# A gate product with tokens as the stationary operand, its nonlinearity in halves, a new order in the last step of a sweep, and an earlier split of one output chunk

## The chip, the cores and the metric

The kernel runs on one core of one Trainium2 chip. The metric is the device time of one execution in microseconds (us). Three timed executions of the kernel before took 1257.67, 1259.69 and 1261.07 us; their median is 1259.69. A further execution was recorded by the hardware profiler, and its trace is what the readings below come from.

Engines: PE is TensorE (matmuls), DVE is VectorE, ACT is ScalarE, POOL is GpSimd, SP is SyncE, which here only issues DMAs.

## What is computed

One encoder layer over 2048 tokens of width 1024 (batch 1). A joint projection feeds two groups of heads, gated linear attention (GLA, both directions) and latent attention (MLA); both are multiplied by a SiLU gate, concatenated, projected, and added to the residual before a layer norm. Cut to what the change touches:

```python
def hybrid_mixer(x, positions, w_in, ..., w_out):
    h = x @ w_in
    (g_q, g_k, g_v, g_gate, g_lr_f, g_lr_b,
     m_cq, m_ckv, m_kr, m_gate) = jnp.split(h, idx, axis=-1)
    o_a = gla_branch(g_q, g_k, g_v, g_gate, ...)      # 512 wide, 4 heads, chunks of 64
    o_b = mla_branch(m_cq, m_ckv, m_kr, m_gate, ...)  # 512 wide, 4 heads
    return jnp.concatenate([o_a, o_b], axis=-1) @ w_out

def mla_branch(c_q, c_kv, k_rope, gate, positions, ...):
    q = (rms_norm(c_q, q_norm_g) @ w_uq).reshape(B, S, 4, 128 + 64)
    kv = (rms_norm(c_kv, kv_norm_g) @ w_ukv).reshape(B, S, 4, 128 + 128)
    ...                                   # rotary parts, dense softmax attention
    return o * jax.nn.silu(gate)

x = layer_norm(DEEPNORM_ALPHA * x + mixed, ln_g, ln_b)
```

Inputs and result are float32. Every large product is made of three passes on operands that are split in a high and a low part (high x high, high x low, low x high); names that end in h and l are these parts.

## The kernel before

The rows of x are 16 chunks of 128 tokens. The kernel has these stages, with the times at which they lie in the profiled execution:

- **The first sweep** (0 to 349 us) goes over the chunks from the last to the first, for the GLA's projections and one direction of its scan. The change does not touch it.
- **The second sweep** (349 to 580 us), `sweep_c`, has 8 steps of two chunks. Each step makes, for both chunks, the MLA projections (`ipm`), the normalised `cq` and `ckv`, their transposes (`tm`), the rotary query `pqr`, the other GLA direction (`Ob`, `og`, `oT`), the absorbed query `pq`, and the gate product `pz` of 512 columns (`c_pz`).
- **The attention** (580 to some 1077 us): 16 blocks, each a head and 512 queries, about 30 us a block.
- **The output** (from some 1060 us): 16 chunks of 128 rows. Each has to be fetched (`OutProj.load`), split into high and low parts (`hi` on ACT, `lo` on POOL), multiplied by the gate (`gate`), multiplied by `w_out`, added to the residual and normalised (`finish`). The layer norm's logarithm and exponential are on ACT.

**The gate product.** `c_pz` computes z transposed: the stationary operand is a block of 128 x 128 of the weights Wz, the moving one the 256 tokens of the step, so that a PSUM tile [128 features, 4 heads, 256 tokens] is filled. A step has 4 heads x 8 slices of the width x 3 passes = 96 matmuls of 128x256, in 8 pieces (n = 0 to 7), which the tables place among the other work. Then `c_gm1` to `c_gm3` (ACT: exp(-z), ln(1 + that), exp of minus that) and `c_gm4` (DVE: times z) make the SiLU on the whole tile (128x1024) in one go, into the SBUF tile `gm`, and `c_sgm` stores it to the scratch `gm_s`. The tile `gm` and the low part of the absorbed query, `qal`, have the same tag and so take turns in one buffer: `gm`'s first writer waits until the store `ql_s<-qal` has landed.

**PSUM.** `pz`, `Ob` and `pq` take turns in the two tiles of the tag "gp". A wait between engines is set per tile, not per part of a tile.

**What sets the order.** For the second sweep every piece of work has a place in a table: `PLACE_C`, with `PLACE_C_FIRST` and `PLACE_C_LAST` for the first and last step. A place is a number of steps after the step's start; where there are two, they are for the step's two chunks. `put` adds step and place, all is sorted by the sum, and `in_order` then fixes that order on each engine:

```python
def put(n, st, fn, *a, j=None):
    last = st == len(steps) - 1
    p = PLACE_C[n]
    p = (last and PLACE_C_LAST.get(n)) or (not st and PLACE_C_FIRST.get(n)) or p
    todo.append((st + (p if j is None else p[j]), len(todo), fn, a))
```

The attention has a sorted list of the same kind. In the output the order in the code is fixed for ACT, POOL and SP (`fixed`), not for PE and DVE. There, `split(c + 2)`, `load(c + 4)`, `product`, `finish` follow each other for each chunk c from 4 on. The work `turn` and `rows` of the last block but one (a turned row of softmax sums, which ACT copies as `rt` to go to the scratch r_s) stands after chunk 6's `finish`.

The GLA's output goes to DRAM as `oa_s`, turned in blocks of 32x32, and `load` puts the blocks in their places with four DMAs for each chunk (`blocks_of`).

Of the kernel before, what the change touches and what calls it, by code (L numbers as in the profile page):

```python
# [9 lines left out]
F32 = mybir.dt.float32  # L10
# [125 lines left out]
STEP_C = ("gm1", "gm2", "gm3", "gm4", "sgm", "pq", "qah", "qal", "sqa")  # L136
# [3 lines left out]
    "ss", "rgl", "rgd", "og", "oT", "soT")  # L140
# [57 lines left out]
    gm1=0.823,  # L198
    gm2=0.832,
    gm3=0.837,  # L200
    gm4=0.845,
# [72 lines left out]
    gm1=0.643,  # L274
    gm2=0.815,
    gm3=0.82,
    gm4=0.83,
# [14 lines left out]
    pqr=(0.749, 1.284),  # L292
    tq=(0.95, 2.1),
    xh=(-0.262, -0.109),
    sqO=(0.15, 0.435),
    rgl=(0.229, 0.457),
    sqm=(0.101, 0.657),
    rml=(0.187, 0.878),
    cq=(0.463, 1.041),
    ckv=(0.35, 1.075),  # L300
# [6 lines left out]
    oT=(0.337, 0.509),  # L307
    oib=(0.063, 0.43),
    ss=(0.166, 0.454),
    rgd=(0.332, 0.461),  # L310
    og=(0.336, 0.508),
    ssm=(0.1025, 0.733),
    rmd=(0.29, 1.022),
    krf=(0.139, 0.6),
    cqTl=(0.598, 1.211),
    ckvTl=(0.88, 1.703),
    qrf=(0.795, 1.556),
    qrTl=(1.081, 2.186),
    xl=(-0.244, 0.3),
# [6 lines left out]
    qrfa=(0.871, 2.029),  # L326
# [3 lines left out]
    lu=(0.281, 0.47),  # L330
# [3 lines left out]
    gm1=1.309,  # L334
    gm2=1.608,
    gm3=1.859,
    gm4=1.953,
# [16 lines left out]
class K:  # L354
# [151 lines left out]
    def run(self):  # L506
        tc, nc, ins = self.tc, self.nc, self.ins
        with ExitStack() as top:
# [9 lines left out]
            self.gm_s = [dp.tile([P, H, QB], F32, name=f"gm_s{b}") for b in range(NQB)]  # L518
# [3 lines left out]
            self.kt_s = [dp.tile([P, H, P], F32, name=f"kt_s{c}") for c in range(NCH)]  # L522
            self.r_s = [dp.tile([1, H, QB], F32, name=f"r_s{b}") for b in range(NQB)]
# [627 lines left out]
    def sweep_c(self):  # L1151


        with ExitStack() as ctx:
# [102 lines left out]
    def c_pz(self, s, n):  # L1257
        last = s["st"] == NCH // 2 - 1
        if n == 0:
            s["pz"] = self.gp.tile([P, H, 256], F32, tag="gp", name=f"pz{s['st']}")  # L1260
        order = [(h, k) for h in range(H) for k in range(NK)]
        if last:
            order = [(h, k) for p in range(2) for k in range(NK) for h in (p, p + 2)]
        x2 = lambda t, k: t[:, k].rearrange("p a t -> p (a t)")
        part = [(h, k, p) for h, k in order[4 * n:4 * n + 4] for p in range(3)]
        if n == 0 and s["st"]:

            part.sort(key=lambda e: e[2] == 1)
        stop = {h: (k, p) for h, k, p in part if k == NK - 1}
        for h, k, p in part:  # L1270
            w, x = ((0, self.xch), (0, self.xcl), (1, self.xch))[p]
            self.nc.tensor.matmul(s["pz"][:, h], self.Wz[k][w][:, h * P:(h + 1) * P], x2(x, k),  # L1272
                                  start=(k == 0 and p == 0), stop=stop.get(h) == (k, p))

    def c_gm1(self, s):
        s["gm"] = self.w1.tile([P, H, 256], F32, tag="gm", name=f"gm{s['st']}")
        self.nc.scalar.activation(s["gm"], s["pz"], AF.Exp, scale=-1.0)

    def c_gm2(self, s):
        self.nc.scalar.activation(s["gm"], s["gm"], AF.Ln, bias=1.0)  # L1280

    def c_gm3(self, s):
        self.nc.scalar.activation(s["gm"], s["gm"], AF.Exp, scale=-1.0)

    def c_gm4(self, s):
        self.nc.vector.tensor_tensor(s["gm"], s["pz"], s["gm"], ALU.mult)
# [4 lines left out]
    def c_sgm(self, s):  # L1291
        b, qs = self.of_step(s)
        self.nc.sync.dma_start(self.gm_s[b][:, :, qs], s["gm"])
# [825 lines left out]
```

## Time and profile before

| | us |
|---|---|
| median of three timed executions | 1259.69 (1257.67 to 1261.07) |
| profiled execution, its own time | 1264.79 |
| span of the profiled execution | 1262.9 |
| PE busy | 1239.1 |
| DVE busy | 896.3 |
| ACT busy | 729.1 |
| POOL busy | 726.5 |

How such a page is read: busy times are of one engine and overlap with the others; an engine with idle time may still hold up another. The views used below are: the chain of waits (from the last instruction back to what released each step), the list of what an engine waited for (total, times, longest), windows (busy time of every engine in a stretch of the span, with PE's granted clock as a share of full speed and the DMA engines' mean busy share), groups of instructions (engine, operation, tile written <- tile read, shape, count, then busy time, mean in ns, idle time before and what ended it), the timeline (start, length, engine, line, operation, and in brackets the idle time before it and what ended that), and DMA groups (count, KB each, us from issue to landing). PE's matmuls are pipelined, so the time of one in a run is the distance from its start to the next one's, not its listed length.

### The profile page before, as it was taken

The numbers are of one execution on the slowest core, as the hardware profiler recorded it, in microseconds if no ns is written. First come the engines' busy times: TensorE is split into PE (matmuls) and PEld (weight loads), VectorE is DVE, ScalarE is ACT, GpSimd is POOL, SyncE is SP. The second block draws the span as 40 slices with busy tenths as digits, with TensorE's granted clock in tenths as the row PEclk, the third lists the DMA queues.
The fourth block names the chain that finished last, engine by engine and source line by source line (L and its number), as shares of the span: only waits on it lengthen the run. The fifth ranks groups of instructions, "written<-read, shape, count | busy, mean of one in ns | idle before, by whom it ended". The sixth has DMA issues, their size and how long they took to land.

```text
span 1262.9 us, 19554 instructions
## 1 busy us (share of the span) xinstructions
PE 1239.1 (98%) x6848; PEld 1089.6 (86%) x6848; DVE 896.3 (71%) x1666; ACT 729.1 (58%) x1149; POOL 726.5 (58%) x443
## 2 busy tenths in 40 slices
PE   7999999999999999999999999999999999999997
PEld 7999999999899999988788888888888888887886
DVE  6635454554565666665899999999999998378767
ACT  6643434444564444544888888888888888411210
POOL 0132323232355556530798888889999999935551
PEclk9999999999999999999999999999999999999999
DMA  8225555555757788868412222202234110487773
GB/s 294 68 84 130 134 143 139 144 139 144 266 180 212 212 247 244 245 184 210 79 28 49 43 50 43 53 15 59 59 93 93 41 42 26 125 206 212 198 210 100
DMA packets 277393, 165.59 MB, mean 131 GB/s; under 512 B 178630, under 2 KB 234830, under 8 KB 277296
## 3 DMA queue, kind: packets, MB, share of 16 engines
q1 hardware_dynamic: 276176, 162.23, 48.3%
q0 software_dynamic: 672, 2.10, 0.4%
q8 instruction: 54, 0.88, 0.3%
q14 instruction: 43, 0.35, 0.1%
q10 hardware_dynamic: 448, 0.03, 0.0%
HBM read 105.54 MB, written 58.75 MB: 130 GB/s over the span
## 4 chain that ended last, share of the span: by engine, by line
PE 84%; DVE 4%; DMA 4%; POOL 2%; issue 2%; ACT 2%; SPq 1%; DVEq 0%; POOLq 0%; ACTq 0%
PE pz L1272 7%; PE ipm L1341 5%; PE pS L1605 5%; PE pS L1607 4%; PE pS L1606 4%; PE pS L1608 4%; PE pS L1609 4%; PE o L421 4%; PE o L419 4%; PE o L420 4%; PE ipa L419 4%; PE ipa L421 4%; PE ipa L420 4%; PE ipg L421 2%; PE ipg L419 2%
## 5 line engine op out<-in xcount | busy, mean ns | idle before, releaser
L371 POOL TENSOR_TENSOR pl<-s,ph 128x1024 fp32r<-128x1024 f32 x128 | 306.8, 2416 | 47.2 <-ACT ph L365 37.0
L1614 ACT ACTIVATE s<-pS 128x1024 f32<-128x1024 f32 x128 | 131.5, 1028 | 52.9 <-PE pS L1609 49.0
L1627 DVE TENSOR_TENSOR rm<-pS,rm 128x512 f32<-128x512 f32 x210 | 144.6, 689 | 18.3 <-ACT s L1614 12.7
L1651 DVE TENSOR_TENSOR s<-s,mb 128x1024 f32<-128x1024 f32 x128 | 151.2, 1213 | 9.0 <-PE mb L1645 8.9
L365 ACT ACTIVATE ph<-s 128x1024 fp32r<-128x1024 f32 x128 | 134.8, 1056 | 15.7 <-PE o L421 15.1
L1655 ACT ACTIVATE s<-s 128x1024 f32<-128x1024 f32 x128 | 131.6, 1051 | 10.3 <-DVE s L1651 9.6
L419 PE MATMUL ipa<-wah,xah 128*128 128x384 f32 (+1 forms) x384 | 129.2, 336 | 6.1 <-ACT wah L365 6.1
L420 PE MATMUL ipa<-wal,xah 128*128 128x384 f32 (+1 forms) x384 | 125.0, 325 | 0.0
L421 PE MATMUL ipa<-wah,xal 128*128 128x384 f32 (+1 forms) x384 | 124.7, 325 | 0.0
L1091 POOL TENSOR_TENSOR Sb<-Sb,Us 64x512 f32<-64x512 f32 x15 | 19.9, 1327 | 171.5 <-DVE Us L1083 162.3
L1605 PE MATMUL pS<-qh,kvT 128*128 128x512 f32 x256 | 102.6, 401 | 0.8 <-DVE rm L1627 0.4
L419 PE MATMUL o<-ph,vh 128*128 128x512 f32 x256 | 100.9, 394 | 0.0
L1607 PE MATMUL pS<-qh,kvT 128*128 128x512 f32 x256 | 100.0, 391 | 0.0
L1606 PE MATMUL pS<-ql,kvT 128*128 128x512 f32 x256 | 100.0, 390 | 0.0
L421 PE MATMUL o<-ph,vl 128*128 128x512 f32 x256 | 99.8, 390 | 0.0
L1608 PE MATMUL pS<-rh,kvT 128*128 128x512 f32 x256 | 99.8, 390 | 0.0
L1609 PE MATMUL pS<-rl,kvT 128*128 128x512 f32 x256 | 99.8, 390 | 0.0
L420 PE MATMUL o<-pl,vh 128*128 128x512 f32 x256 | 99.7, 389 | 0.0
L1678 DVE TENSOR_TENSOR ap<-ap,s 128x512 f32<-128x512 f32 x120 | 82.9, 691 | 2.7 <-ACT s L1655 0.7
L419 PEld LDWEIGHTS ipa<-wah,xah 128*128 128x128 f32 x384 | 73.3, 191 | 9.3 <-ACT wah L365 6.4
L371 POOL TENSOR_TENSOR ol<-of,oh 128x512 fp32r<-128x512 f32 x32 | 42.5, 1328 | 59.8 <-ACT oh L365 47.4
L1272 PE MATMUL pz<-xch,wzh 128*128 128x256 f32 x256 | 73.4, 290 | 1.4 <-DVE og L1529 1.3
(308 smaller groups left out, 3404.9 us busy)
## 6 DMA issues: line engine op xcount, KB each, us to landing
xcf<-xT_dram SPq DMA_DIRECT2D x16, 512.0 KB, 5.5
xr<-x_dram SPq DMA_DIRECT2D x16, 512.0 KB, 6.0
out_dram<-rr SPq DMA_DIRECT2D x32, 256.0 KB, 3.5
xaf<-xT_dram SPq DMA_DIRECT2D x14, 512.0 KB, 4.2
oib<-oi_s SPq DMA_DIRECT2D x16, 256.0 KB, 4.9
qdb<-qd_s SPq DMA_DIRECT2D x16, 256.0 KB, 3.5
SU<-su_s SPq DMA_DIRECT2D x16, 256.0 KB, 5.0
ub<-u_s SPq DMA_DIRECT2D x16, 256.0 KB, 4.1
```

Of the source, the lines that this page charges most:

```text
L371: return e.tensor_tensor(dst, src, hi.bitcast(F32), ALU.subtract).ins
L419: mm(out, ah, bh, start=start, stop=False)
L420: mm(out, ah, bl, start=False, stop=False)
L421: mm(out, al, bh, start=False, stop=stop)
L1272: self.nc.tensor.matmul(s["pz"][:, h], self.Wz[k][w][:, h * P:(h + 1) * P], x2(x, k), start=(k == 0 and p == 0), stop=stop.get(h) == (k, p))
L1605: mm(ps[:, e], kh, qh, start=True, stop=False)
L1606: mm(ps[:, e], kh, ql, start=False, stop=False)
L1607: mm(ps[:, e], kl, qh, start=False, stop=False)
L1608: mm(ps[:, e], kr, rh, start=False, stop=False)
L1609: mm(ps[:, e], kr, rl, start=False, stop=True)
L1627: V.tensor_tensor(d["rm"], src[:, e], d["rm"], ALU.max)
L1651: V.tensor_tensor(s, s, d["mb"][:, None, :].to_broadcast([P, 2, QB]), ALU.subtract)
```

## The change

Six things change together.

1. `c_pz` computes z with tokens in rows. The stationary operand is a chunk's x (128 x 128), the moving one 512 columns of Wz. One half of the tile [128, 2, 512] belongs to each chunk; a step has 48 matmuls of 128x512. Pieces 0 to 3 are the first chunk, 4 to 7 the second.
2. `gm1` to `gm4` are pieces of a chunk, not of a step: each works on 128x512. `gm4` writes its product back to PSUM, and a new DVE piece `gmx` transposes it in blocks of 32x32 into `gm`.
3. `qal` is two tiles of 128x512 under another tag, "og", with two DVE instructions and two stores, and no longer shares `gm`'s buffer.
4. `gm_s` gets the layout of `oa_s`. A new function `place_blocks` copies, during the attention, both from DRAM to a new DRAM scratch `og_s`, with eight DMAs for each chunk, in which the 32x32 blocks are put in their places. `load` then takes one DMA for each of the two instead of four and one.
5. The last step's table has new places for `rml`, `rmd`, `ssm`, `sqm`, `cq`, `ckv`, `oib`, `sqO`, `ss`, `rgl`, `rgd`, `og`, `oT`, `pqr`, `qrf`, `krf`, `lu` and `xl`, and a table `PLACE_C_PRE` changes some of the step before.
6. In the output, chunk 6 is split ahead of chunk 3's `finish`, and `turn` and `rows` of the last block but one stand ahead of chunk 6's `finish`.

```diff
@@ tables
+PLACE_C_PRE = dict(
+    cqTl=(0.758, 1.185),
+    tq=(1.44, 1.56),
...
+    soT=(1.119, 1.3),
+)
-STEP_C = ("gm1", "gm2", "gm3", "gm4", "sgm", "pq", "qah", "qal", "sqa")
+STEP_C = ("sgm", "pq", "qah", "qal", "sqa")
@@ PLACE_C
-    gm1=0.823,
+    gm1=(0.45, 0.823),
...
+    gmx=(0.76, 0.835),
@@ PLACE_C_LAST
-    rml=(0.187, 0.878),
-    cq=(0.463, 1.041),
+    rml=(0.187, 0.535),
+    cq=(0.4275, 0.61),
...
@@ scratch
-            self.gm_s = [dp.tile([P, H, QB], F32, name=f"gm_s{b}") for b in range(NQB)]
+            self.gm_s = [dp.tile([2, H, P, P], F32, name=f"gm_s{s}") for s in range(NCH // 2)]
+            self.og_s = [dp.tile([P, 2, H, P], F32, name=f"og_s{c}") for c in range(NCH)]
@@ put
-                p = PLACE_C[n]
+                p = st == len(steps) - 2 and PLACE_C_PRE.get(n) or PLACE_C[n]
@@ c_pz
-            s["pz"] = self.gp.tile([P, H, 256], F32, tag="gp", name=f"pz{s['st']}")
...
-        for h, k, p in part:
-            w, x = ((0, self.xch), (0, self.xcl), (1, self.xch))[p]
-            self.nc.tensor.matmul(s["pz"][:, h], self.Wz[k][w][:, h * P:(h + 1) * P], x2(x, k),
-                                  start=(k == 0 and p == 0), stop=stop.get(h) == (k, p))
+            s["pz"] = self.gp.tile([P, 2, 512], F32, tag="gp", name=f"pz{s['st']}")
+        j, half = divmod(n, 4)
+        for k in (2 * half, 2 * half + 1):
+            xh, xl = self.xch[:, k, j], self.xcl[:, k, j]
+            self.mm3(s["pz"][:, j], xh, xl, self.Wz[k][0], self.Wz[k][1], start=(k == 0), stop=(k == NK - 1))
@@ gate
+    def gm(self, d):
+        s, j = d["step"], d["j"]
+        if "gm" not in s:
+            s["gm"] = self.w1.tile([P, 2, 512], F32, tag="gm", name=f"gm{s['st']}")
+        return s["gm"][:, j], s["pz"][:, j]
...
-        self.nc.vector.tensor_tensor(s["gm"], s["pz"], s["gm"], ALU.mult)
+    def c_gm4(self, d):
+        gm, pz = self.gm(d)
+        self.nc.vector.tensor_tensor(pz, pz, gm, ALU.mult)
+    def c_gmx(self, d):
+        self.nc.vector.transpose(*self.gm(d))
@@ qal
-        s["ql"] = self.w1.tile([P, H, 256], F32R, tag="gm", name=f"qal{s['st']}")
-        self.lo(s["ql"], s["pq"], s["qh"])
+        s["ql"] = []
+        for n in range(2):
+            hs = slice(2 * n, 2 * n + 2)
+            s["ql"].append(self.w1.tile([P, 2, 256], F32R, tag="og", name=f"qal{s['st']}_{n}", bufs=2))
+            self.lo(s["ql"][n], s["pq"][:, hs], s["qh"][:, hs])
@@ attention
+    def place_blocks(self, c):
+        for n, scr in enumerate((self.oa_s[c], self.gm_s[c // 2][c % 2])):
+            for r, src in self.blocks_of(scr.rearrange("h p (m t) -> h p m t", t=32)):
+                self.nc.sync.dma_start(self.og_s[c][r, n].rearrange("p h (b t) -> p (h b) t", t=32), src)
+            for c in range(NCH):
+                put(NP * min(c, nb - 2) + 6.05, self.place_blocks, c)
@@ output
+                    if c == 3:
+                        split(6)
                     op.finish(rest[c])
...
-                    split(c + 2)
+                    if c > 4:
+                        split(c + 2)
...
                     op.product(rest[c])
+                    if c == 6:
+                        with self.after(*last.values()):
+                            turn(nb - 2)
+                        rows(nb - 2)
                     op.finish(rest[c])
...
-                    if c == 6:
-                        turn(nb - 2)
-                        rows(nb - 2)
@@ OutProj.load
-        for r, src in kern.blocks_of(kern.oa_s[c].rearrange("h p (m t) -> h p m t", t=32)):
-            nc.sync.dma_start(of[r, 0].rearrange("p h (b t) -> p (h b) t", t=32), src)
-        nc.sync.dma_start(gr[:, 0], kern.gm_s[b][:, :, cs])
+        nc.sync.dma_start(of[:, 0], kern.og_s[c][:, 0])
+        nc.sync.dma_start(gr[:, 0], kern.og_s[c][:, 1])
```

How the order moves, at three places. Rows name the line, the operation, the tile written <- tiles read (the number after the tile's name is its step or chunk, the last one only a count) and the shape.

DVE, in the middle of the second sweep (the gate of step 5 stands between the work on steps 4 and 5). Before:

```order
L1452 STREAM_TRANSPOSE qrx9_6086<-qrf9_5970 128x256
L371 TENSOR_TENSOR qal4_6088<-pq4_5991,qah4_6028 128x1024
L371 TENSOR_TENSOR qrT4_5869<-qrx9_6086,qrT4_5869 128x256
L371 TENSOR_TENSOR cqT_l5_6095<-tm10_6059,cqT_h5_6094 128x2x128
L1286 TENSOR_TENSOR gm5_6133<-pz5_5881,gm5_6133 128x1024
L1546 TENSOR_TENSOR krf11_6139<-ipm11_6102,cos_257 128x64
```

and after:

```order
L1474 STREAM_TRANSPOSE qrx9_5864<-qrf9_5774 128x256
L384 TENSOR_TENSOR qal4_0_5866<-pq4_5789,qah4_5830 128x512
L384 TENSOR_TENSOR qal4_1_5868<-pq4_5789,qah4_5830 128x512
L384 TENSOR_TENSOR qrT4_5691<-qrx9_5864,qrT4_5691 128x256
L1299 TENSOR_TENSOR pz5_5703<-pz5_5703,gm5_5820 128x512
L384 TENSOR_TENSOR cqT_l5_5875<-tm10_5849,cqT_h5_5874 128x2x128
L1303 STREAM_TRANSPOSE gm5_5820<-pz5_5703 128x512
L1299 TENSOR_TENSOR pz5_5703<-pz5_5703,gm5_5820 128x512
L1303 STREAM_TRANSPOSE gm5_5820<-pz5_5703 128x512
L1568 TENSOR_TENSOR krf11_5922<-ipm11_5883,cos_277 128x64
```

One product has become two products and two transposes, the first product ahead of `cqT_l`, and `qal` is two instructions.

ACT, in the last step, after the change (before, the gate's pass gm1 on the whole tile stood behind all of these rows):

```order
L1386 ACTIVATE cq15_6602<-ipm15_6398,rm15_r_6569 128x256
L378 ACTIVATE qrT6_6532<-qrx13_6572 128x256
L378 ACTIVATE kvT_3912<-tm14_6551 128x128 x2
L378 ACTIVATE krs15_6618<-krf15_6593 128x64
L1287 ACTIVATE gm7_6626<-pz7_6574 128x512
L378 ACTIVATE vh_3913<-ckv14_6493 128x128
L1291 ACTIVATE gm7_6626<-gm7_6626 128x512
```

The first pass on the gate of step 7's first half now stands behind `cq` of chunk 15, and ahead of the casts for the values.

ACT, in the output. Before:

```order
L365 ACTIVATE oh5_1_11955<-of5_11882 128x512
L432 ACTIVATE ln2_l_11981<-u2_11976 128x1
L433 ACTIVATE ln2_y_11984<-ln2_l_11981 128x1
L432 ACTIVATE ln3_l_12006<-u3_12001 128x1
L433 ACTIVATE ln3_y_12009<-ln3_l_12006 128x1
L365 ACTIVATE oh6_0_12019<-of6_11901 128x512
```

and after:

```order
L378 ACTIVATE oh5_1_11770<-of5_11703 128x512
L445 ACTIVATE ln2_l_11793<-u2_11788 128x1
L446 ACTIVATE ln2_y_11796<-ln2_l_11793 128x1
L378 ACTIVATE oh6_0_11812<-of6_11719 128x512
L378 ACTIVATE oh6_1_11818<-of6_11719 128x512
L445 ACTIVATE ln3_l_11828<-u3_11823 128x1
L446 ACTIVATE ln3_y_11831<-ln3_l_11828 128x1
```

Chunk 6's split (`oh6`) has moved ahead of chunk 3's layer norm.

More of the change, by code (lines that the diff above doesn't have):

```diff
@@ L139 @@
     "tq", "qrTh", "qrTl", "Sf1", "Sf2", "M", "Ob", "oib", "sqO",
[L140 removed]
+    "ss", "rgl", "rgd", "og", "oT", "soT", "gm1", "gm2", "gm3", "gm4", "gmx")
 FETCH_C = ("lx", "xh", "xl")
@@ L273 @@
     pz=(-0.249, -0.195, -0.111, -0.018, 0.405, 0.452, 0.485, 0.622),
[L274 to L277, printed above, removed]
+    gm1=(0.623, 0.643),
+    gm2=(0.6231, 0.815),
+    gm3=(0.6232, 0.82),
+    gm4=(0.65, 0.83),
+    gmx=(0.81, 0.835),
     sgm=1.056,
@@ L306 @@
     qrTh=(1.065, 2.174),
[L307 to L314, printed above, removed]
+    oT=(0.4285, 0.432),
+    oib=(0.063, 0.426),
+    ss=(0.188, 0.428),
+    rgd=(0.25, 0.43),
+    og=(0.26, 0.431),
+    ssm=(0.1025, 0.53),
+    rmd=(0.427, 0.605),
+    krf=(0.24, 0.6),
     cqTl=(0.598, 1.211),
     ckvTl=(0.88, 1.703),
-    qrf=(0.795, 1.556),
+    qrf=(0.875, 1.556),
     qrTl=(1.081, 2.186),
-    xl=(-0.244, 0.3),
+    xl=(-0.244, 0.2),
     M=(-0.531, -0.11),
@@ L333 @@
     pz=(0.572, 0.578, 0.707, 0.845, 0.918, 1.023, 1.1, 1.22),
[L334 to L337, printed above, removed]
+    gm1=(0.855, 1.309),
+    gm2=(0.91, 1.608),
+    gm3=(1.2, 1.859),
+    gm4=(1.26, 1.953),
+    gmx=(1.265, 1.954),
     sgm=2.042,
```

61 lines of the change are left out of this document (30 added, 31 removed).

## The prediction

> **What bounds the kernel now.** I read the shares and the chain of waits first, then what TensorE (PE) waited for, then the windows around those waits.
>
> ```profile
> PE 1239.1 (98%) x6848; PEld 1089.6 (86%) x6848; DVE 896.3 (71%) x1666; ACT 729.1 (58%) x1149; POOL 726.5 (58%) x443
> PE 84%; DVE 4%; DMA 4%; POOL 2%; issue 2%; ACT 2%; SPq 1%; DVEq 0%; POOLq 0%; ACTq 0%
> PE pz L1272 <- DVE og L1529: 1.3, 2, 0.9
> PE pqr L421 <- DVE cqT_l L371: 1.3, 1, 1.3
> PE ipm L1341 <- POOL xcl L371: 1.0, 1, 1.0
> PE pmb L421 <- POOL ol L371: 1.0, 1, 1.0
> PE rt L1747 <- ACT rt L1753: 0.8, 1, 0.8
> PE pmb L419 <- ACT oh L365: 0.3, 1, 0.3
> PE pq L419 <- DVE og L1529: 0.3, 1, 0.3
> ```
>
> PE is busy for 98% of the span and holds 84% of the last chain. So the time falls only through less work on PE, or through one of the short waits listed. What VectorE (DVE) and ScalarE (ACT) gain or lose counts only where it makes or ends such a wait.
>
> ```profile
> 408.00:412.40 4.40, 2.69 (x21) 2.27 (x20) 3.64 (x18) 2.71 (x14) 3.61 (x3) 1.00 0.98 303
> 412.40:415.80 3.40, 3.40 (x19) 3.40 (x18) 3.31 (x13) 1.82 (x8) 2.87 (x4) 0.51 0.72 178
> 440.30:468.00 27.70, 27.70 (x204) 27.00 (x201) 17.48 (x63) 13.90 (x37) 15.20 (x17) 1.00 0.82 237
> 544.20:580.50 36.30, 33.51 (x246) 31.89 (x245) 24.35 (x95) 17.09 (x54) 9.47 (x15) 1.00 0.70 183
> 612.00:1060.00 448.00, 448.00 (x2038) 368.62 (x2036) 407.15 (x554) 381.96 (x408) 407.16 (x177) 1.00 0.23 50
> ```
>
> Columns: length, then busy time of PE, PE's loads, DVE, ACT, POOL, then granted clock, DMA share and GB/s. A steady step of the second sweep (440.3) is PE from end to end, with DVE 17.5 of 27.7 us busy. Losses sit in the third step (408 to 415.8: PE stands, then runs at clock 0.51) and in the last (544.2: 36.3 us with 33.5 busy). In the attention (612 to 1060) PE never stops.
>
> **Part 1: the gate product on PE.** Before, 96 matmuls of 256 columns a step; now 48 of 512. The start-to-start times, from one run of each form:
>
> ```profile
> 355.81 0.28 PE L1272 MATMUL pz<-xch,wzh 128*128 128x256 f32 x1
> ...
> 361.09 0.28 PE L1272 MATMUL pz<-xch,wzl 128*128 128x256 f32 x1
> 339.29 0.39 PE L419 MATMUL ipg<-wgh,xbh 128*128 128x512 f32 x1
> ...
> 348.58 0.39 PE L421 MATMUL ipg<-wgh,xbl 128*128 128x512 f32 x1
> ```
>
> 5.28 us over 44 intervals is 0.120 us; 9.29 over 41 is 0.2266. A step saves 96 x 0.120 - 48 x 0.2266 = 0.64 us, eight steps 5.1: **-5.0**. The columns streamed are the same, so this is only the fixed part of a matmul. The rival price is that operands now swapped (the token tile stationary) cost more to load: bound 0 to -5.
>
> The Trainium skill, "TensorE: Matmul & The Clock Gate", section "Wait — 56ns, not 53.3ns?", gives N / 2.4 GHz plus about 2.5 ns from one warm matmul to the next. By that estimate 109.2 and 215.8 ns, so 0.12 us a step and 1.0 in all. The trace disagrees: both forms stand 11 ns above it, and per pair it is 13 ns that fall away, not 2.5.
>
> **Part 2: the wait in the third step.** Before, gm shared its buffer with qal, whose store ql_s had to land first. It was issued 7.2 us before ACT could go on, while the DMA engines were at 0.98 (the profile names qr_s, queued behind it):
>
> ```profile
> 393.15 0.52 SPq L1314 DMA_DIRECT2D ql_s<-qal  x1
> 400.31 1.03 ACT L1277 ACTIVATE gm<-pz 128x1024 f32<-128x1024 f32 x1 [2.46 <-DMA qr_s<-qrT]
> 403.55 1.22 DVE L1286 TENSOR_TENSOR gm<-pz,gm 128x1024 f32<-128x1024 f32 x1 [8.78 <-ACT gm L1283]
> 409.80 0.44 PE L1413 MATMUL tm<-ident,cq 128*128 128x128 f32 x2 [0.83 <-ACT cq L1364]
> 411.11 0.39 PE L1272 MATMUL pz<-xch,wzh 128*128 128x256 f32 x1 [0.88 <-DVE og L1529]
> ```
>
> ACT was held 2.46 us, and everything behind on DVE came late: 8.8 us later PE waits 0.83 and 0.88. So this chain has a slack of 2.46 - 0.83 = **1.6 us** against PE. The next 3.4 us run at clock 0.51, which costs another 1.7. The change gives qal two tiles of another pool tag, so that hold can't recur: 0.83 + 0.88 + 1.7 = **-3.4**. Bounds: 0, if the timed executions never had it (one profile shows it once in eight steps), to -3.4.
>
> The same page of the Trainium skill, section "What's actually happening", has a free-running window of about 3.4 us after which the clock halves; the row agrees with the length (3.40 us at 0.51), though the waits ahead of it were under 1 us each, not a whole idle window.
>
> **Part 3: the gate chain on ACT and DVE.**
>
> ```profile
> L1535 DVE STREAM_TRANSPOSE oT<-og 128x512 f32<-128x512 f32 x16 | 11.4, 711 | 0.5
> L829 DVE STREAM_TRANSPOSE qx<-ipa 128x256 f32<-128x256 f32 x12 | 5.3, 440 | 0.0
> L1563 DVE TENSOR_TENSOR gs<-ipg,gs 128x512 f32<-128x512 f32 x14 | 9.7, 690 | 27.4 <-ACT gs L1561 27.4
> L1559 ACT ACTIVATE gs<-gs 128x512 f32<-128x512 f32 x14 | 8.8, 632 | 0.4
> L1280 ACT ACTIVATE gm<-gm 128x1024 f32<-128x1024 f32 x8 | 8.5, 1060 | 0.2
> ```
>
> DVE per step: 2 x 0.69 for the product and 2 x 0.71 for the new transposes instead of one 1.22 (the 403.55 row); with qal in two, 2 x 0.69 for about 1.2. That is 1.6 + 0.2 = 1.8 us more, into 10.2 us that DVE has free. The new transpose reads PSUM; the row of qx, a transpose out of PSUM of half the size in 0.440, against 0.711 for oT out of SBUF, lets me keep 0.71. ACT: 6 x 0.62 for 3 x 1.05, 0.6 more.
>
> What counts is the chain. After PE's last gate matmul it was 3 x 1.05 + 1.22 = 4.4 us. Dependences go by whole tile, so now: the first half's product (0.69) waits for PE's last matmul, its transpose (0.71), only then ACT's three passes on the second half (1.9), product and transpose (1.4): 4.7 us. +0.3, inside the slack of 1.6: nothing in steps 2 to 6, **+0.6** in all for handovers, bounds 0 to +2. PE too has a new wait: its first matmul of the second half needs ACT's first pass on the first half (0.6); 24 matmuls of pq (2.9 us) stand between, so it is covered. If that cover went, it would cost 8 x 0.6.
>
> In step 1 no cover is left: PE's pq waits there already for DVE's og (the 0.3 in the list of waits). DVE's four operations in place of one put og up to 1.6 us later; part of them lies in time in which DVE now idles, so I take **+1.2**, bounds 0 to +2.
>
> **Part 4: the last step.** The waits on pqr, xcl and the last 0.44 of pz go: 1.3 + 1.0 + 0.4 (the pz row's 1.3 less 0.88) = **2.8** in the window of 544.2. New ones come. With the second half's start PE needs ACT's pass gm1, which now stands in ACT's order behind cq15, and cq15 behind DVE's normalising rows of chunk 15.
>
> ```profile
> 562.54 1.02 ACT L365 ACTIVATE qah<-pq 128x1024 fp32r<-128x1024 f32 x1
> 566.30 0.41 DVE L371 TENSOR_TENSOR cqT_l<-tm,cqT_h 128x256 fp32r<-128x256 f32 x1
> 572.43 0.47 ACT L1364 ACTIVATE cq<-ipm,rm_r 128x256 f32<-128x256 f32 x1 [3.50 <-DVE rm_r L446]
> ```
>
> From pq's last matmul: qah 1.0, the two qal 1.4, cqT_l 0.4, krf and rope about 0.5, four small rows about 0.7, cq 0.5, three casts about 1.0, gm1 0.6, together 6.1 (the "abouts" are estimates, from the small DVE and ACT rows above), and some 1.5 for six handovers (0.2 to 0.3 each): 7.6. PE's cover is 24 x 0.227 + 6 x 0.12 + two small ones = 6.5. So it waits about 1.1. The order also puts pqr and pq close behind cqT_l and og; I take 0.9 for these. -2.8 + 2.0 = **-0.8**, bounds -2.8 to +2.
>
> **Part 5: chunk 6 and the copied row.**
>
> ```profile
> 1122.26 3.03 SPq L1956 DMA_DIRECT2D of<-oa_s x4
> 1139.19 0.20 ACT L432 ACTIVATE ln_l<-u 128x1 f32<-128x1 f32 x1 [7.86 <-DVE u L2042]
> 1139.59 0.63 ACT L365 ACTIVATE oh<-of 128x512 fp32r<-128x512 f32 x1
> 1144.61 0.63 ACT L365 ACTIVATE oh<-of 128x512 fp32r<-128x512 f32 x1 [4.39 <-POOL of L1965]
> 1168.51 0.25 ACT L1753 ACTIVATE rt<-rt 4x128 f32<-4x128 f32 x1
> ```
>
> Chunk 6's data had been fetched from 1122; its split (oh) stood behind ACT's layer-norm row, which waited 7.86 us. Split first, POOL starts up to 8 us sooner: PE's 0.3 and 1.0 go. ACT's row copy, put ahead of the layer norm, ends the 0.85. **-2.1**. What is late next is that layer norm, which no matmul reads. Bounds 0 to -2.1.
>
> **Part 6: the regrouped copies.**
>
> ```profile
> of<-oa_s SPq DMA_DIRECT2D x64, 64.0 KB, 3.9
> DMA packets 277393, 165.59 MB, mean 131 GB/s; under 512 B 178630, under 2 KB 234830, under 8 KB 277296
> ```
>
> 128 copies of 64 KB inside DRAM, in pieces of 128 B, run during the attention, where DMA's share is 0.23; 64 such reads go from the output. They hold 65,536 pieces, over a third of what the whole kernel has under 512 B. SP issues eight per block of 30 us, at about 0.8 us each by the 1122.26 row. Zero, hidden under PE; bounds 0 to +3 (if q's fetches come late).
>
> **Sum.** -5.0 - 3.4 + 0.6 + 1.2 - 0.8 - 2.1 = -9.5. Against the profiled execution, 1264.8 us with 1262.9 of span, that gives 1255.3. It lies 5.1 above the timed median (1259.7). If the third step's stall is in the timed runs too, they come to 1250.2; if the profile alone had it, to 1253.6. The gap of 5.1 looks like such a chance stall, so I take nearer the second: **1253**.
>
> **Rivals.**
> *Gain by half.* The operands' swap gives 1.0 instead of 5.0, or DVE's 1.8 us per step reappear as waits of about 0.5 each in eight steps. 1253 + 4 = 1257. For it: steps 0, 1 and the last have shown waits on DVE; against: the intervals above. For the first of these the Trainium skill's rule speaks; nothing in the rows does.
> *The stall's whole price returns.* If all timed runs had it and the last step's order works fully, 1250. It was once in eight steps, with DMA's share at 0.98, so it may be load.
> *Slower.* The chain through PE, DVE, ACT and DVE outgrows its slack in the middle steps. Point of decision: 1.6 us over 4.4. If a transpose out of PSUM took 1.6 us, not 0.71, the chain is 6.5, 0.5 over; at 2 us it is 7.3, 1.3 over in each of seven steps, +9. The third step of before shows what then comes behind such a wait: 3.4 us at half clock, 1.7 lost. If that falls on every second step, +6 more: 1268. For it: PE, DVE and ACT write and read the same PSUM tile in turn, which no row has; against: qx's 0.440.
> *The new tags change nothing*: the hold in the third step came of the full DMA queues (0.98) and finds another wait, the gm buffer's own store for one. Then -3.4 falls away: 1258.7 against the profiled 1264.8, and 1253.6 for timed runs that never had the stall.
>
> **Chances.** Forecast (1250.5 to 1255.9) 0.55; 1250 or below 0.15; half 0.18; slower 0.12. A measurement of this kernel tells 0.3% (3.8 us) from no change. So faster (below 1255.9) 0.70, same 0.18, slower 0.12. Range 1248.5 to 1259.5, which leaves out the slower case and little below; the forecast's own is 1250.5 to 1255.9.
>
> **What would show it.** Right: pz intervals of 0.227 in the profile after; a steady step of 27.1 us; no clock of 0.5 between 400 and 420; no PE wait on oh or rt in the output. Wrong: PE waiting in every step on DVE's og or on ACT's gm, a transpose from PSUM far over 0.75, PE gaps in the attention behind fetches of q, or pz intervals above 0.235.

## The result, and the profile after

| | before | after |
|---|---|---|
| median of six executions, us | 1259.97 | 1254.95 |
| lowest and highest | 1257.67, 1261.96 | 1252.82, 1255.32 |
| profiled execution: own time, span | 1264.79, 1262.9 | 1253.20, 1251.4 |

The ratio after to before is 0.9956, with a 95% interval of 0.9945 to 0.9967: faster by 0.44%, 5.0 us by the medians. A second series on another chip gave 0.9947 (0.9934 to 0.9960). The forecast was 1253.0, in a range of 1248.5 to 1259.5.

The page's shares, the chain of waits, and what PE waited for, after:

```profile
PE 1231.4 (98%) x6464; PEld 1066.7 (85%) x6464; DVE 910.5 (73%) x1698; ACT 732.5 (59%) x1173; POOL 727.8 (58%) x443
PE 90%; DVE 3%; ACT 2%; issue 2%; DMA 2%; POOL 1%; SPq 0%; DVEq 0%; POOLq 0%; ACTq 0%
PE pz L432 <- ACT gm L1287: 1.8, 1, 1.8
PE pz L432 <- DVE og L1551: 1.1, 1, 1.1
PE mb L1673 <- DVE mc L1666: 0.8, 1, 0.8
PE pq L432 <- DVE og L1551: 0.6, 2, 0.4
```

PE is still the bound, and the waits on oh, ol, rt, cq, cqT_l and xcl are gone from its list. Two are new or larger: on ACT's gm in the last step, and on DVE's og in the second.

Windows of the second sweep, the attention and the output, after (columns as in the prediction); and the output's window of before:

```profile
372.50:402.10 29.60, 28.08 (x156) 24.53 (x154) 21.39 (x75) 14.12 (x40) 16.15 (x18) 1.00 0.67 209
402.10:429.30 27.20, 27.20 (x156) 24.46 (x154) 18.94 (x67) 14.46 (x41) 15.30 (x16) 1.00 0.83 243
429.30:456.40 27.10, 27.10 (x154) 24.36 (x153) 19.44 (x67) 14.36 (x40) 15.13 (x16) 1.00 0.85 242
537.90:572.00 34.10, 32.07 (x191) 28.75 (x190) 24.42 (x92) 16.55 (x55) 8.61 (x13) 1.00 0.76 195
612.00:1046.00 434.00, 434.00 (x1973) 357.49 (x1972) 394.24 (x537) 368.68 (x393) 393.66 (x171) 1.00 0.34 68
1082.50:1226.50 144.00, 144.00 (x639) 119.01 (x638) 104.67 (x187) 23.41 (x60) 82.69 (x55) 1.00 0.61 202
```

```profile
1091.20:1238.10 146.90, 144.75 (x640) 118.80 (x639) 101.58 (x179) 24.01 (x59) 81.01 (x55) 1.00 0.72 194
```

The third step (402.1) is now a plain step of 27.2 us, without a stop and at full clock. The output takes 144.0 us for 146.9, PE without a gap. The attention never stops, though DMA's share there has gone from 0.23 to 0.34.

The second sweep by steps, from the first `ipm` matmul of a step's first chunk to that of the next step's (the last one ends with the first score matmul), in us. The rows below the first two are experiments that come later; "half clock" says where a stretch of 3.4 us at clock 0.5 lies in it, and all other times in the table are free of one:

| kernel | step 1 | 2 | 3 | 4 to 7, each | 8 | sum |
|---|---|---|---|---|---|---|
| before | 25.68 | 28.50 | 31.35, half clock | 27.66 | 35.54 | 231.70 |
| after | 25.29 | 29.55 | 27.17 | 27.17 | 34.11 | 224.78 |
| after, second series | 25.29 | 29.59 | 27.17 | 27.17 | 35.71, half clock | 226.43 |
| three parts (e10) | 25.68 | 28.51 | 27.66 | 27.66 | 33.41 | 225.90 |
| three parts and form (e11) | 25.14 | 28.25 | 27.17 | 27.17 | 33.41 | 222.63 |
| gm1 first (e8) | 25.29 | 29.59 | 27.17 | 27.17 | 32.47 | 223.19 |
| whole gate (e9) | 25.64 | 29.26 | 27.31 | 27.31 to 27.35 | 33.32 | 224.83 |

The profiled executions differ by 11.5 us, the timed ones by 5.0. Of the 11.5, 6.9 lie in the second sweep, 2.8 in the output, and 1.6 in the first sweep (348.81 to 347.24 us), which the change does not touch (it took 346.8 to 348.8 us in the profiles of this study). The profile of before was an unlucky one: it has the half clock in the third step and the longest first sweep of all.

### The profile page after: what moved, and what is told of

It reads as the page before. It is cut to its first block, busy times and chain, and to the rows that moved or that the text cites. A ratio compares the mean times of both kernels' runs of the same rounds, so it can differ in the third digit from the quotient of the medians.

```text
span 1251.4 us, 18903 instructions
## 1 busy us (share of the span) xinstructions
PE 1231.4 (98%) x6464; PEld 1066.7 (85%) x6464; DVE 910.5 (73%) x1698; ACT 732.5 (59%) x1173; POOL 727.8 (58%) x443
## 4 chain that ended last, share of the span: by engine, by line
PE 90%; DVE 3%; ACT 2%; issue 2%; DMA 2%; POOL 1%; SPq 0%; DVEq 0%; POOLq 0%; ACTq 0%
PE ipm L1363 5%; PE o L432 5%; PE o L434 5%; PE o L433 5%; PE pS L1633 5%; PE pS L1635 5%; PE pS L1634 5%; PE pS L1637 5%; PE pS L1636 5%; PE ipa L432 4%; PE ipa L434 4%; PE ipa L433 4%; PE po L433 3%; PE po L434 3%; PE po L432 3%; PE ipg L434 2%
## 5 line engine op out<-in xcount | busy, mean ns | idle before, releaser
L433 PEld LDWEIGHTS ipa<-wal,xah 128*128 128x128 f32 x384 | 72.7, 189 | 1.9 <-DVE wal L384 1.4
```

Of the source, the lines that this page charges most:

```text
L433: mm(out, ah, bl, start=False, stop=False)
```

## The experiments

Each changes the kernel before or the changed kernel, in one part or in several together. Ratios are against the kernel before, timed on the same chip; "by the ratio" is the ratio turned into us of some 1260. An excess, where an expectation speaks of one, is the time by which a wait makes a run of matmuls longer, so PE's idle time and its slow restart together.

**e1: the form of the gate product alone.** To the kernel before:

```diff
-            self.nc.tensor.matmul(s["pz"][:, h], self.Wz[k][w][:, h * P:(h + 1) * P], x2(x, k), ...)
+        j, half = divmod(n, 4)
+        out = s["pz"].rearrange("p (a b) t -> p a (b t)", a=2)[:, j]
+        for k in (2 * half, 2 * half + 1):
+            xh, xl = self.xch[:, k, j], self.xcl[:, k, j]
+            self.mm3(out, xh, xl, self.Wz[k][0], self.Wz[k][1], start=(k == 0), stop=(k == NK - 1))
```

> The kernel before with only the gate product in the new form: 48 matmuls of 128x512 a step with the token tile stationary, in place of 96 of 128x256. The rest of the gate works as before on the whole tile, on values that are not turned, so the transposition of the gate is left out and the gate's values stand in the wrong places of the result. Theory (a fixed part of some 13 ns per pair of matmuls falls away): 0.55 to 0.64 us a step, -4.4 to -5.1 us in all, so about 1255, and 27.1 us for a steady step. Rival (the page's start-to-start times, 109.2 and 215.8 ns): 0.12 a step, -1.0 in all. Second rival (swapped operands load worse): 0 or more.

Measured: ratio 0.9967 (0.9955 to 0.9979), 1256.62 for 1261.46, so -4.2 by the ratio. Each steady step takes 27.17 for 27.66 us and so gains 0.49; the first gains 0.54, the second 0.23, the last 0.12, since there waits take the rest. The rival of 0.12 in each step falls. Not all of the -4.2 need be the form's: the output, which this kernel leaves as it was, took 144.9 us in its profile for 146.9, without the waits on oh and ol. e11 against e10, further down, is the cleaner measure.

**e2: the output edits alone** (chunk 6's split ahead of chunk 3's layer norm, the row's copy ahead of chunk 6's).

```diff
+                    if c == 3:
+                        split(6)
                     op.finish(rest[c])
...
+                    if c == 6:
+                        with self.after(*last.values()):
+                            turn(nb - 2)
+                        rows(nb - 2)
                     op.finish(rest[c])
```

> The kernel before with only the output edits: chunk 6 split ahead of chunk 3's layer norm, and the last block but one's row turned and copied ahead of chunk 6's layer norm. Theory (three waits of PE, on oh, ol and rt, with their excess 0.45 + 1.17 + 1.01 in the trace of before, end for good): -2.1 to -2.6 us, about 1257.6, no PE wait in the output. Rival (the time comes back as another wait behind, or the waits were a chance of the profiled execution): 0, about 1260.

Measured: 0.9983 (0.9972 to 0.9994), 1258.88, so -2.1 by the ratio. The output's window is free of gaps:

```profile
1088.70:1232.70 144.00, 144.00 (x640) 119.01 (x639) 99.25 (x179) 24.12 (x59) 81.62 (x55) 1.00 0.72 199
```

**e3: the query's low part in its own tiles.**

```diff
-        s["ql"] = self.w1.tile([P, H, 256], F32R, tag="gm", name=f"qal{s['st']}")
+            s["ql"].append(self.w1.tile([P, 2, 256], F32R, tag="og", name=f"qal{s['st']}_{n}", bufs=2))
```

> The kernel before with only the low part of the absorbed query in two tiles of the other tag, so that the gate's buffer never waits for its store. Theory (the stop in the third step and the half clock behind it were a chance of the one profiled execution): 0 within 0.5 us, about 1260, since timed executions seldom have it. Rival (each execution has it): -3.4 to -3.7, about 1256.4. Second rival (two more DVE instructions and one more DMA a step cost): +0.2 to +1.

Measured: 0.9986 (0.9975 to 0.9997), 1259.79, so -1.8 by the ratio: between the theory of 0 and the rival of -3.4. ACT's first pass in the third step now starts with no wait:

```profile
395.56 1.06 ACT L365 ACTIVATE xch<-xcf 128x1024 fp32r<-128x1024 f32 x1 [2.28 <-PE pz L1272]
396.53 1.01 ACT L1277 ACTIVATE gm<-pz 128x1024 f32<-128x1024 f32 x1
```

The profiles of the five kernels with the shared buffer show the third step at 31.35 (before), 28.07 (e1), 29.33 (e2), 31.65 (e4) and 30.30 (e12), with ACT's first gate pass there held for 1.9 to 3.3 us until stores have landed; e3 and all other kernels, in which the buffer isn't shared, show a plain step. So the stop is in every profile with the shared buffer, and the buffer is its cause. What changes from one to the next is its length and whether the half clock follows. (e3's own profile has the half clock in the last step, which takes 36.46 us there for 35.54, so its span understates the gain.)

**e4: the last step's places alone**, with the table for the step before it and the gate's own places left.

```diff
-    cq=(0.463, 1.041),
+    cq=(0.4275, 0.61),
...
+                p = st == len(steps) - 2 and PLACE_C_PRE.get(n) or PLACE_C[n]
```

> The kernel before with only the new places of the last step and of the one before it, the gate's own places left as they were. Theory (of the change's -0.9 in the last step, 3.28 us of excess go and 2.35 come, of which 1.98 are the gate's new wait, which is not in this kernel): -2.3 to -2.9 us, about 1257.4. Rival (the waits only move, since pqr and pq now stand close behind their sources): -0.5 to +0.5.

Measured: 0.9986 (0.9975 to 0.9996), 1259.08, so -1.8 by the ratio. The last step takes 33.36 us for 35.54 (e10, with the same places, 33.41). The waits on pqr, xcl and og in the last step end, and a shorter one on ckv (0.62 us) comes.

**The changed kernel once more**, on another chip.

> The changed kernel once more, on the chip of the next three. The four parts tried alone sum to -4.8 - 2.6 - 1.7 - 2.4 = -11.5 us by their medians, the change as a whole gave -5.0. Theory (its parts that were not tried alone, the gate in halves with its transposes and the copies, cost some 5 us together): a ratio of 0.995 to 0.997 again. Rival (the two chips differ, and the parts do add up): 0.991 to 0.993.

Measured: 0.9947 (0.9934 to 0.9960), 1254.01. Its profile has the half clock close behind the new wait on gm. The window from 557 holds the wait, the next one the clock:

```profile
557.00:563.40 6.40, 4.59 (x23) 3.74 (x23) 4.64 (x19) 3.00 (x12) 2.00 (x5) 1.00 0.93 294
563.40:566.80 3.40, 3.40 (x13) 2.67 (x11) 0.49 (x2) 0.67 (x2) 0.01 (x1) 0.51 0.80 190
```

**e6: the changed kernel without the copies.**

```diff
-        nc.sync.dma_start(of[:, 0], kern.og_s[c][:, 0])
-        nc.sync.dma_start(gr[:, 0], kern.og_s[c][:, 1])
+        for n, (scr, dst) in enumerate(((kern.oa_s[c], of), (kern.gm_s[c // 2][c % 2], gr))):
+            for r, src in kern.blocks_of(scr.rearrange("h p (m t) -> h p m t", t=32)):
+                nc.sync.dma_start(dst[r, 0].rearrange("p h (b t) -> p (h b) t", t=32), src)
```

> The changed kernel without the copies inside DRAM: the output fetches both the GLA's result and the gate in 32x32 blocks, with four DMAs each instead of one each. Theory (the copies lie under an attention in which PE never stops): within 0.5 us of the changed kernel, or up to +1 where the output's fetches (eight block DMAs for each chunk, 0.8 us each on SP) come late. Rival (the copies hold up q's fetches, or their traffic falls into the half clock): -2 to -5 against the changed kernel.

Measured: 1.0007 (0.9997 to 1.0017), 1261.78, 7.8 us slower than the changed kernel beside it; neither expectation. The second sweep is that of the changed kernel (224.80), the output takes 152 us instead of 144, with these waits and the fetches of a chunk on SP:

```profile
PE pmb L432 <- DVE rr L2065: 4.4, 4, 2.7
PE rt L1775 <- DVE rc L1763: 0.8, 1, 0.8
1126.45 3.73 SPq L1990 DMA_DIRECT2D of<-oa_s  x4
1130.30 3.31 SPq L1990 DMA_DIRECT2D gr<-gm_s  x4
1133.65 0.49 SPq L1991 DMA_DIRECT2D gr<-r_s  x1
1134.18 0.53 SPq L1992 DMA_DIRECT2D of<-ob_s  x1
1154.24 0.62 SPq L2011 DMA_DIRECT2D xr<-x_dram  x1
1160.55 0.69 DVE L2065 SCALAR_TENSOR_TENSOR rr<-xr,pmb 128x512 f32<-128x512 f32 x1 [9.48 <-DMA xr<-x_dram]
1162.80:1166.20 3.40, 3.40 (x10) 2.63 (x8) 3.23 (x9) 1.00 (x3) 1.59 (x2) 0.50 0.62 130
```

SP spends 8.1 us on the fetches of the chunk shown, with the residual's fetch and the stores still to issue, and PE needs about 9 us for a chunk. The last three rows show how this reaches PE: from 1139.7 on SP issued sixteen block fetches, then only, at 1154.24, the residual's fetch xr. DVE stood for 9.48 us until that had landed, PE for 2.72 us for DVE, and shortly behind this wait PE ran 3.4 us at half clock. Waits of 5.2 us and the half clock's 1.7 are most of the 7.9 us by which the output is longer. So the copies are what pays for the gate's new layout. Another order on SP, with the residual's fetch ahead of the blocks, was not tried.

**e8: ACT's gm1 ahead of cq of chunk 15.** To the changed kernel:

```diff
-    cq=(0.4275, 0.61),
+    cq=(0.4275, 0.856),
-    krsh=(0.33, 0.782),
+    krsh=(0.33, 0.857),
```

> The changed kernel with ACT's pass gm1 on the last step's first half ahead of cq of chunk 15 and of krs15, in a stretch in which ACT waits for DVE (2.43 us ahead of cq in the trace of the changed kernel). Theory (PE's wait of 1.8 on gm1, 1.98 of excess, is only a matter of ACT's order): no such wait, -1.5 to -2 us against the changed kernel. Rival (the next wait behind takes it over, on tm of chunk 15 or at the attention's start): 0 to -0.5.

Measured: 0.9936 (0.9924 to 0.9948), 1252.77, for 0.9947 and 1254.01 of the changed kernel beside it. The last step takes 32.47 for 34.11 us, and PE no longer waits on gm:

```profile
PE ipa L432 <- ACT wah L378: 5.4, 1, 5.4
PE pz L432 <- DVE og L1551: 1.1, 1, 1.1
PE mb L1673 <- DVE mc L1666: 0.8, 1, 0.8
```

In the trace the theory holds (-1.64 us). In time it is -1.2 by the medians; the intervals of the two overlap. By its median it is the fastest kernel here that leaves nothing out.

**e9: the gate's passes and product on the whole tile**, then the two transposes. To the changed kernel:

```diff
-STEP_C = ("sgm", "pq", "qah", "qal", "sqa")
+STEP_C = ("gm1", "gm2", "gm3", "gm4", "gmx", "sgm", "pq", "qah", "qal", "sqa")
...
+    def c_gm4(self, s):
+        self.nc.vector.tensor_tensor(s["pz"], s["pz"], s["gm"], ALU.mult)
+    def c_gmx(self, s):
+        for j in range(2):
+            self.nc.vector.transpose(s["gm"][:, j], s["pz"][:, j])
```

> The changed kernel with the gate's passes and product on the whole tile again (three passes and one product of 128x1024, then the two transposes), in the places of the kernel before. Theory (halves bring the gate no gain, and cost PE's wait on gm1 and ACT 0.6 us a step, while the chain behind PE's last gate matmul of 3.15 + 1.22 + 1.4 = 5.8 us stays inside its slack of 1.6 over 4.4): -1 to -3 against the changed kernel. Rival (the chain outgrows its slack, so PE stops in each middle step, 0.3 to 1 us each and at times at half clock): +2 to +10.

Measured: 0.9941 (0.9929 to 0.9954), 1253.41: not told apart from the changed kernel. PE stops in no middle step, even with a chain of 5.8 us, so the rival falls; but each of them takes 0.14 us more, and the last one 0.8 less. Halves and whole come out even, and the gain of 1 to 3 that the theory expected doesn't show. The second step takes 29.26 us, 1.0 more than in e11, which has no transposes: so of the changed kernel's loss there most comes with the transposes, and only 0.3 with the halves.

**e10: e2, e3 and e4 together**, no new gate and no copies.

> The kernel before with three parts of the change together: the output edits, the query's low part in tiles of the other tag, and the last step's places; the gate as before, no copies. Theory (the parts sit in different stretches and add up): by ratios -2.1 - 1.8 - 1.8 = -5.7, by medians up to -6.7, so a ratio of 0.9947 to 0.9955, about the whole change's gain; then the new gate as a whole nets near nothing. Rival (they overlap, since the third step's stop and the last step's waits both pass through the half clock): -3 to -4.

Measured: 0.9956 (0.9943 to 0.9970), 1255.38 for 1260.61: -5.5 by the ratio, the sum of the three (-5.7).

**e11: the same, with the new form of e1.**

> The same three parts and the gate product in its new form, with the rest of the gate on the whole tile and without the transposition, so that the gate's values stand in the wrong places of the result; no copies. Theory (the form gives 0.49 us a step, as steady steps of 27.17 for 27.66 show, and what the changed kernel lacks of the sum goes into the transposes and halves of the gate): another -3.9 to -4.4 against the three parts, -10 against before, ratio 0.991 to 0.993. Rival (the form's gain is already spent inside the second sweep, as other waits on DVE's og): no more than -2 against the three parts.

Measured: 0.9926 (0.9911 to 0.9940), 1251.59: 3.8 us below e10. By steps the form gives 0.54, 0.26 and five times 0.49, but nothing in the last, where a wait on ckv grows: 3.3 in all. It is what the change would be if the gate's turning (transposes, halves, copies) cost nothing. From it to the changed kernel stand +1.30 in the second step, +0.70 in the last (+2.30 with the half clock) and +0.15 in the first: 2.15 of the second sweep. In time, the ratio of 0.9926 against the changed kernel's 0.9947 and 0.9956 is 2.6 to 3.8 us.

**e7: the changed kernel with the last step's old places.**

```diff
-    cq=(0.4275, 0.61),
+    cq=(0.463, 1.041),
...
+PLACE_C_PRE = dict()
```

> The changed kernel with the last step's old places (the gate's own new places kept) and without the table for the step before it. Theory (the old waits on pqr, xcl and og come back, 3.3 us of excess, but ACT then has gm1 ahead of cq of chunk 15 and the gate's wait of 1.98 goes): +1 to +1.5 against the changed kernel, 0.9955 to 0.996 against before. Rival (the gate's wait stays): +3.

Measured: 0.9963 (0.9948 to 0.9977), 1256.03, so +0.9 to +2.0 against the changed kernel's two ratios; the intervals overlap. In the trace it is more: the last step takes 36.65 us for 34.11, +2.5, with the old waits on pqr (1.33 us), xcl (1.03) and og (0.90) back. The wait on gm shrinks from 1.82 to 0.69 us and doesn't go, so the theory holds only in part.

**e12: the copies alone**, for the GLA's result, in the kernel before.

```diff
+            for c in range(NCH):
+                put(NP * min(c, nb - 2) + 6.05, self.place_blocks, c)
...
-        for r, src in kern.blocks_of(kern.oa_s[c].rearrange("h p (m t) -> h p m t", t=32)):
-            nc.sync.dma_start(of[r, 0].rearrange("p h (b t) -> p (h b) t", t=32), src)
+        nc.sync.dma_start(of[:, 0], kern.og_s[c])
```

> The kernel before with only the copies: the GLA's result is put into its final layout inside DRAM during the attention (64 of the 128 DMAs, the gate keeps its old layout and needs none), and the output fetches it with one DMA a chunk instead of four. Theory (hidden under an attention in which PE never stops, and the output's fetches were not late before): 0 within 0.6 us. Rival (fewer DMAs on SP in the output end waits): -1 to -2.5. Second rival (traffic in the attention holds up q's fetches): +1 to +3.

Measured: 0.9987 (0.9974 to 0.9999), 1259.63, so -1.6 by the ratio. The output has no gap, with its order untouched:

```profile
1089.80:1233.80 144.00, 144.00 (x640) 119.03 (x639) 105.79 (x187) 23.42 (x60) 83.22 (x55) 1.00 0.63 202
```

The traces say how. DVE's residual of chunk 3, in before and here:

```profile
1135.35 1.29 DVE L2032 SCALAR_TENSOR_TENSOR rr<-xr,po 128x512 f32<-128x512 f32 x2 [1.78 <-DMA out_dram<-rr]
1129.85 1.28 DVE L2038 SCALAR_TENSOR_TENSOR rr<-xr,po 128x512 f32<-128x512 f32 x2
```

In before DVE waits there until a store of the result, which SP issued behind the block fetches, has landed; the layer norm that held up chunk 6's split is late by this. With one fetch for four the store goes out 32.0 us into the output instead of 37.1, and the wait is gone. So the first rival holds: fetches in one piece end the same three waits that e2 ends by order. The two parts are not added: with either, the output takes 144.0 us, as it does with both. One caution: e1's profile lacks this DVE wait too, and PE's waits on oh and ol with it, though nothing in its output was changed. So two of the three waits are not in every execution of the old output, and e12's gain, whose interval ends at 0.9999, rests on one profile.

## Why the prediction held, step by step

**The time.** 1254.95 lies within the forecast's own range (1250.5 to 1255.9), 2 us above its value. That it lies so near is in part luck. The form's term was 1.2 to 1.7 too large, and the last step's new wait cost more than forecast and at times brings the half clock. Against these, the third step's stop, worth 1.8, had been taken as nearly absent from the timed executions, and the 0.6 for handovers did not come.

**Part 1, the form: -5.0 forecast, -3.3 in the trace (e11 against e10), -3.8 timed.** The direction and the cause stand: a steady step gains 0.49 us. By the start-to-start times of the Trainium skill ("TensorE: Matmul & The Clock Gate", section "Wait — 56ns, not 53.3ns?") it would have been 0.12; the trace disagrees. The size is off for two reasons. A run of the new matmuls, in a middle step of the changed kernel:

```profile
444.30 0.39 PE L432 MATMUL pz<-wzh,xch 128*128 128x512 f32 x1
...
446.82 0.39 PE L434 MATMUL pz<-wzh,xcl 128*128 128x512 f32 x1
```

2.52 us over 11 intervals is 0.229, where 0.2266 was taken from another product; 48 of them take back 0.12 of the 0.64, about 1 us in eight steps. The rest is that the second and the last step have waits, so PE's saving there goes into waiting longer (0.26 and 0 gained in place of 0.49).

**Part 2, the stop in the third step: -3.4 as the upper bound, -1.8 measured (e3).** That gm and qal in separate buffers end it was right. The step that failed is "The gap of 5.1 looks like such a chance stall": the stop was in all five profiles with the shared buffer. Only its length and the half clock behind it varied. Had the stop been taken as fixed and the clock as chance, the term was 0.83 + 0.88 = 1.7, about what the timing gives.

**Part 3, the gate chain.** (The prediction counts steps from 0, the table from 1.) Right in the middle steps: 27.17 us in the changed kernel and in e11, which has neither transposes nor halves, so DVE's extra work is free there. The transposes out of PSUM were sized rightly (gm<-pz), and so was the product:

```profile
L1303 DVE STREAM_TRANSPOSE gm<-pz 128x512 f32<-128x512 f32 x16 | 11.4, 710 | 0.3
L1299 DVE TENSOR_TENSOR pz<-pz,gm 128x512 f32<-128x512 f32 x16 | 11.2, 700 | 35.2 <-PE pz L434 18.2 <-ACT gm L1295 13.2 <-ACT gm L1287 3.7
```

0.710 against the forecast's 0.71, and DVE's 1.2 for the second step came as 1.30, though not on pq: its wait on og is 0.39 us in the changed kernel and in e11 alike, while the wait of pz on og went from 0.06 to 1.11. The +0.6 for handovers did not come. The slower rival, which needed a transpose of 1.6 us or more, falls with this row.

**Part 4, the last step: -0.8 forecast.** From 35.54 to 34.11 is -1.43, or -0.9 without the 0.49 that the form gives a free step. The new wait was named rightly (PE's second half on gm1, behind cq15), but costs 1.98 of excess (1.82 idle) instead of 1.1; the 0.9 allowed beside it came as 0.4. The forecast let the chain start with qah right behind pq's last matmul (552.5 in the changed kernel). In ACT's order a cast of the rotary query stands ahead of qah, and it waited for DVE:

```profile
555.25 0.42 ACT L378 ACTIVATE qrT<-qrx 128x256 fp32r<-128x256 f32 x1 [2.79 <-DVE qrx L1474]
555.58 1.01 ACT L378 ACTIVATE qah<-pq 128x1024 fp32r<-128x1024 f32 x1
561.81 0.60 ACT L1287 ACTIVATE gm<-pz 128x512 f32<-128x512 f32 x1
```

So the chain began 3.1 us late. From qah's start to gm1's end it then took 6.8 us, less than the 7.6 forecast (no row shows the 0.2 to 0.3 us that it allowed for each handover), and PE's cover was 8.0 instead of 6.5: 3.1 + 6.8 - 8.0 is 1.9, about the excess measured. What the sum also left out: this wait can bring the half clock, 1.6 us more, as the second series shows. This is where the changed kernel leaves 1.64 us, which e8 takes by order alone.

**Part 5, the output: -2.1 forecast, -2.8 in the trace, -2.1 timed (e2).** Right; the gaps alone were 2.1, and PE's restart adds some 0.15 behind each (excess 0.45, 1.17 and 1.01 against idle times of 0.29, 1.00 and 0.85).

**Part 6, the copies: 0 forecast.** Right for the attention, whose time did not move (474.9 before, 474.7 after) with DMA's share at 0.34. Not seen was that one fetch instead of four ends the output's waits by itself (e12), so parts 5 and 6 fix the same thing twice. And not seen was what the copies are there for: without them the new layout costs 7.8 us (e6).

**The rivals.** "Gain by half" was the nearest: order, buffer and output give -5.5 (e10), the form 3.8 more (e11), and the turning of the gate gives 2.6 to 3.8 back, through the second and the last step, as that rival's second mechanism had it, though not in every step. The traces show 2.15 of this; the half clock behind the wait on gm comes on top in some executions (see the last section). "The stall's whole price returns" had it right that the stop is no chance, but not all have the half clock, and the form gave less. "The new tags change nothing" falls with e3.

## What to carry to other kernels

A stop that one profile shows should be looked for in the profile of every variant before it is called chance: its cause may be fixed, and only its length and the clock behind it vary. When an operation is cut in pieces that share a tile, the new waits stand where the order of the steady state doesn't apply: here in the second and the last step. And an edit is worth what it adds to the others: here order and fetch size each removed the same three waits.

## What the runs showed of the hardware that was not expected

PE fell to half clock for 3.41 us at a time behind short stops, in six of the fourteen profiles. Where PE had waited 1.81 us on gm (second series), the clock was 0.50 from 563.48 to 566.89; behind the same wait in the changed kernel's first profile (1.82) and in e6 (1.81) it stayed full. In the third step it was half behind 0.83 + 0.88 us of idle time in before, but full behind 1.27 + 0.88 in e12.

What decides, as far as the traces show, is where the stop lies. In each profile all changes of the granted clock lie whole multiples of 3.413 us apart, so there is a fixed grid, which starts elsewhere in each execution. In before the clock rises at 13.08 us, falls at 412.44 (117 x 3.413 later), rises at 415.85 and falls at 1258.94 (247 x 3.413 later), when PE is done. In the first profile of the changed kernel it rises at 8.48 and falls at 1247.51, 363 x 3.413 later. The gm wait, in the stretches of this grid, in the second series (two rows) and in the first profile (two rows):

```profile
560.07:563.48 3.41, 1.60 (x8) 1.23 (x7) 1.90 (x7) 2.46 (x8) 1.48 (x3) 1.00 1.01 332
563.48:566.89 3.41, 3.41 (x12) 2.71 (x10) 0.42 (x1) 0.67 (x2) 0.00 (x0) 0.50 0.81 188
558.02:561.43 3.41, 2.63 (x15) 2.10 (x13) 2.52 (x11) 0.95 (x5) 0.32 (x1) 1.00 0.93 281
561.43:564.85 3.42, 2.38 (x10) 1.99 (x11) 2.22 (x7) 2.38 (x9) 1.47 (x3) 1.00 1.00 298
```

In the second series the whole stop lies in one stretch, PE is idle for 1.81 of 3.41 us, and the next stretch runs at half clock. In the first profile a boundary cuts the stop in two, 0.78 and 1.03 us, and nothing follows. All stretches of the fourteen profiles with the most idle time, from the clock's first rise to 7 us before the end:

| profile | stretch | PE idle in it, us | the next stretch |
|---|---|---|---|
| e4 | 406.54 to 409.96 | 2.02 | half clock |
| e6 | 1159.36 to 1162.78 | 1.93 | half clock |
| e12 | 551.55 to 554.97 | 1.86 | half clock |
| second series | 560.07 to 563.48 | 1.81 | half clock |
| before | 409.03 to 412.44 | 1.65 | half clock |
| e3 | 549.66 to 553.08 | 1.64 | half clock |
| e1 | 545.50 to 548.91 | 1.64 | full |
| e2 | 550.70 to 554.12 | 1.52 | full |
| all others | | 1.41 or less | full |

So in these traces a stretch that is idle for some 1.64 us or more, about half of it, is followed by one at half clock. No run was made to move a stop on the grid; this is read from the fourteen profiles. It also gives an estimate of what the gm wait costs beyond itself: if its place on the grid is even, 1.65 of its 1.82 us fall into one stretch in (3.41 - 1.82 + 2 x 0.17) / 3.41 = 0.57 of the executions, at 1.6 us each some 0.9 us on average. With the 2.15 of the traces that makes about 3.1, within the 2.6 to 3.8 by which e11 is faster than the changed kernel.

The Trainium skill ("TensorE: Matmul & The Clock Gate", section "What's actually happening") has a free-running window of about 3.4 us, which agrees with the grid, and at least one idle window ahead of the half clock, which does not: here a window that was idle for about half was enough.

A transpose of 128x512 in 32x32 blocks takes DVE 0.710 us out of PSUM (`gm` from `pz`) and 0.711 out of SBUF (`oT`): at this size the source has no price.
